# Opening of a fused attention block: order of the rotated key's copies, of the latent evictions, and eight extra matmuls at the start

## The chip, the cores and the metric

The kernel runs on one core of one Trainium2 chip. The metric is the device time of one execution in microseconds (us). Three timed runs of the kernel before the change took 625.54, 625.70 and 627.62 us; the median is 625.70 us. Below, 0.5% of that (3.1 us) is taken as the smallest difference that counts as faster or slower.

## The reference

One decoder layer on 512 tokens with 16 learned meta tokens ahead of them, model width 1024. Two attention branches of 16 heads run on the same normed input and are merged by gates:

```
u = rmsnorm(h, pre_norm_g[l])
proj = u @ w_in[l]
(cq, ckv, k_pe_raw, z_mla, fq, fk, fv, f_logit, z_fox, gate_a, gate_b) = jnp.split(proj, split_idx, axis=-1)
q = (rmsnorm(cq, ...) @ w_uq[l])...          # per head 64 plain + 32 rotary
kv = (rmsnorm(ckv, ...) @ w_ukv[l])...       # per head 64 key + 64 value
k_pe = rope(k_pe_raw, pos)[:, None]          # one rotated key for all heads
q_m = jnp.concatenate([q_nope, rope(q_pe, pos)], axis=-1)
k_m = jnp.concatenate([k_nope, broadcast k_pe], axis=-1)
o_mla = causal_block_attention(q_m, k_m, v_mla, MLA_SCALE)
log_f = log_sigmoid(f_logit + fox_forget_b); cum = jnp.cumsum(log_f)
o_fox = causal_block_attention(fq, fk, fv, FOX_SCALE, cum)
mixed = (sigmoid(gate_a) * y_mla + sigmoid(gate_b) * y_fox) @ w_out[l]
h = h + rmsnorm(mixed, post_norm_g[l])
```

## The kernel before, in words

Every float32 product is made of three passes in float32r: each operand is split into a high half and a low half, and high x high, low x high and high x low are summed in PSUM. So each weight block of 128x1024 goes through three steps: a DMA into `wraw` (three buffers), a copy of the high half on ScalarE (`wh`, line 127), and a subtraction on GpSimd (`wl`, line 102). Each result leaves PSUM the same way: ScalarE copies the high half, VectorE subtracts the low one (`split_lo`, line 102).

The work has an opening, sixteen attention stages (head pairs, forgetting branch and latent branch in turn) whose gaps are filled with projections, a merge, and an output product. Only the opening is touched. TensorE's order is written out by hand; the other four engines' orders come from a scheduler that follows priorities, and each engine runs its list strictly in order.

The opening, for five row tiles t (four of 128 tokens, and tile 4 of 16 meta tokens): load `ht`; sum of squares and scale into `hn`; transpose on TensorE (`pt`, by `turn`, line 351) and evict as `uTh` (ScalarE, line 372) and `uTl` (VectorE, line 369). `small` (line 387) multiplies with the narrow weights `wsh`/`wsl` into `psm` (cq, ckv, raw rotary key, forget logits). `back` (line 399) norms that and rotates the key into `sm`. `latent` (line 424) transposes `sm` on TensorE into `pc`, **of which there is one buffer**, and empties it by four evictions: `cTh` (ScalarE, line 433), `cTl` (VectorE, line 434 through 102), `kpT` (the rotated key, ScalarE, line 435) and `fT` (forget logits, ScalarE, line 436). The next tile's `pc` transposes wait for all four.

Then come, in TensorE's order: the forgetting branch's first queries `fq` and keys `fk` (two halves), the first rotary queries `ppe` (two halves, from cTh/cTl), the first values `v` (two halves), four steps of a gate `pg`, and the first scores `st`. These products take turns on three PSUM banks (`accp`), so each starts only once the result three before it has left: the second `ppe` waits for the first `hlk` (VectorE's split of `fk`), and `v` waits for the second `hlk`.

Beside that, VectorE has: `hlq` and `hlk` (splits of fq, fk); `KPH`, four copies of the rotated key to four partition groups (line 560), and `KPL`, two subtractions (line 563 through 102); the forget sums `fa` (lines 506 and 507, the scan) and `ch` (line 511), which go by DMA into `CT`, an operand of the first scores; the rotation products `pt<-ppe` (line 623); the values' maxima `vsc` and splits `vh` (lines 668 to 690); and `sf`, the masked scores out of PSUM (line 755). The first scores have four `st` banks; after four tiles they wait for `sf`. GpSimd has the `wl` splits, the setup of `maskt`, `vh`, `pn` and `KPL` (lines 545 to 561), and the rest of the rotation of ppe (lines 628 to 631), whose casts into `gT` take the memory in which `kpT` and `ch` lay, so they wait for the last reader of `kpT`.

Of the kernel before, what the change touches and what calls it, by code (L numbers as in the profile page):

```python
# [23 lines left out]
S = 512  # L24
META = 16
L = S + META
NH = 16
# [27 lines left out]
def block_kernel(ctx: ExitStack, tc: tile.TileContext, x, meta_tokens, pre_norm_g, w_in, fox_forget_b,  # L55
# [45 lines left out]
    def split_lo(eng, lo, src, hi):  # L101
        eng.tensor_tensor(out=lo, in0=src, in1=f32(hi), op=ALU.subtract)  # L102
# [158 lines left out]
    with ExitStack() as ph:  # L261
# [63 lines left out]
        hns, sts, pts0 = {}, {}, {}  # L325
# [73 lines left out]
        def back(t):  # L399
# [6 lines left out]
            for a, b, i in both:  # L406

                nc.scalar.activation(sm[:rows, a:b], psm[:rows, a:b], AF.Square, scale=(b - a) ** -0.5,
                                     accum_out=st2[:rows, i : i + 1])
# [14 lines left out]
        def latent(t, sm):  # L424
# [8 lines left out]
            nc.scalar.copy(cTh[:, i0:3, ds], pc[:, i0:3, :rows])  # L433
            split_lo(nc.vector, cTl[:, i0:3, ds], pc[:, i0:3, :rows], cTh[:, i0:3, ds])
            nc.scalar.copy(kpT[:, ds], pc[0:ROPE, 3, :rows])
            nc.scalar.activation(fT[:, ds], pc[ROPE : ROPE + NH, 3, :rows], AF.Identity, bias=fb)
# [5 lines left out]
        free = lambda ins: ins  # L442
        gps = ppt.tile([128, 4, 128], F32, tag="pt", name="gps")
# [20 lines left out]
        for c in (2, 3):  # L464
# [33 lines left out]
        qk = q_fox(0) + k_fox(0)  # L498
        run(qk[:7])
# [19 lines left out]
        run(qk[7:])  # L519
# [14 lines left out]
    with ExitStack() as att:  # L534
# [24 lines left out]
        for r in range(4):  # L559
            nc.vector.tensor_copy(KP[0][32 * r : 32 * r + 32], kpT)  # L560
        nc.gpsimd.memset(f32(KP[1]), 0.0)
# [3 lines left out]
        gpool = gctx.enter_context(tc.tile_pool(name="gpool", bufs=1, side="right"))  # L565
        gT = [gpool.tile([128, KD, S], F32, tag=n, name=n) for n in ("gT0", "gT1")]
# [25 lines left out]
        def pe_unit(g):  # L592
            if g == 0:
                r0, tt = (p.rearrange("p a b -> p (a b)")[:, 0 : 8 * S].bitcast(F32).rearrange("p (c s) -> p c s", c=4)
                          for p in pts)
            else:
                r0, tt = gT[0][:, 4:8], gT[1][:, 4:8]
            rp = r0[:, 0:2]

            rr = [r0[:, 2:4], tt[:, 2:4]] if g else [t[:, 4:6] for t in gT]  # L600
            if g == 0:
                nc.sync.dma_start(rp, rope_pe)
# [8 lines left out]
            def srcs():  # L611
                if g:

                    tc.keep_in_program_order(nc.sync.dma_start(rp, rope_pe))
                return [wuqh[:, k, 8 * g : 8 * g + 8, NOPE + 16 * x : NOPE + 16 * x + 16]
                        for x in range(2) for k in range(2)]

            for xi in range(2):
                get = (lambda: half(1)) if xi else weights(srcs, lambda ws: half(0, ws))

                def done(i, ps, xi=xi):
                    for cs in range(2):
                        nc.vector.tensor_tensor(out=tt[:, 2 * xi + cs], in0=ps, in1=rp[:, cs], op=ALU.mult)
                out += unit(f"ppe{g}{xi}", get, cq_act, 2, REAL, done)

            def rest(x):

                nc.gpsimd.tensor_tensor(out=tt[:, x], in0=tt[:, x], in1=tt[:, 3 - x], op=(ALU.subtract, ALU.add)[x])
                hi, lo = rr[x][:, 0], rr[x][:, 1]
# [4 lines left out]
                else:  # L634

                    for h in range(2):
                        for i in range(2):
                            r = 64 * h + 32 * i + 16 * x
                            dma(f32(QP[r : r + 16]), rr[x][16 * h : 16 * h + 16, i])

            def store(x, a, b):
                for i in range(2):
                    dma(qpe_dram[8 * g + a : 8 * g + b, i, x], rr[x][16 * a : 16 * b, i])
# [193 lines left out]
        pe, rest0, store0 = pe_unit(0)  # L837
        pe_rest = [(0, lambda x=x: rest0(x)) for x in range(2)]
        g = gate_unit()
        first = pe + v + [(0, in_order)] + g[:4]  # L840
# [23 lines left out]
        run(first)  # L864
# [190 lines left out]
```

## Time and profile before

| what | value |
|---|---|
| median of the three timed runs | 625.70 us |
| profiled execution: span from first to last instruction | 622.1 us |
| median less span (what lies around the instructions) | 3.6 us |
| TensorE busy | 599.9 us, 96% of the span |
| VectorE, ScalarE, GpSimd busy | 315.4, 330.8, 265.5 us |
| TensorE busy in the first 74 us | 62.1 us |
| chain of work that ended last | TensorE 86%, VectorE 5%, ScalarE 4% |

The profile lists no device time of its own for the profiled execution; its span is set beside the timed runs. Times in the trace are us from the span's start. A row of the timeline gives start, duration, engine, line, operation, out<-in, shapes, count, and in brackets the idle time before it and what ended that.

### The profile page before, as it was taken

How to read it: one execution, taken by the hardware profiler on the slowest of the kernel's cores; microseconds unless marked ns; L12 is line 12 of the kernel's file. 1: busy time of each engine (PE TensorE's matmuls, PEld its weight loads, DVE VectorE, ACT ScalarE, POOL GpSimd, SP SyncE). 2: the span in 40 equal slices, each digit the busy share in tenths (PEclk: the TensorE clock that was granted, in tenths of full speed). 3: DMA queues.
4: the chain of work that ended last, by engine and by line, in shares of the span. 5: the costliest groups of instructions: out<-in, count | busy, mean ns of one | idle time of the engine just before them, and what ended most of it. 6: DMA issues, size and time to landing. Idle time of an engine off the chain costs nothing.

```text
span 622.1 us, 11008 instructions
## 1 busy us (share of the span) xinstructions
PE 599.9 (96%) x3811; PEld 507.3 (82%) x3811; DVE 315.4 (51%) x922; ACT 330.8 (53%) x757; POOL 265.5 (43%) x270
## 2 busy tenths in 40 slices
PE   5997999799999999999999999999999999999996
PEld 5886789689889789888888898887888888888885
DVE  3848647555765764674675657627321122024034
ACT  7755745655764864774676657656322222232321
POOL 4307535352346543344443523542744444444610
PEclk9999999899999999999999999999999999999999
DMA  9422589969798787878579697871433332333602
GB/s 289 99 76 53 120 178 142 242 141 190 145 186 161 149 208 154 172 167 204 140 161 174 145 169 159 187 168 40 136 102 101 102 93 79 100 103 115 257 34 102
DMA packets 223512, 89.31 MB, mean 144 GB/s; under 512 B 141708, under 2 KB 216852, under 8 KB 223456
## 3 DMA queue, kind: packets, MB, share of 16 engines
q1 hardware_dynamic: 223456, 88.61, 61.9%
q8 instruction: 30, 0.49, 0.3%
q14 instruction: 26, 0.21, 0.1%
HBM read 54.43 MB, written 4.00 MB: 94 GB/s over the span
## 4 chain that ended last, share of the span: by engine, by line
PE 86%; DVE 5%; ACT 4%; issue 2%; DMA 1%; SPq 0%; POOL 0%; DVEq 0%; ACTq 0%
PE z L96 14%; PE pg L96 14%; PE py L96 14%; PE v L96 9%; PE fq L96 7%; PE po L96 7%; PE fk L96 7%; PE st L96 5%; PE ov L96 3%; PE psm L96 3%; DVE sf L755 2%; PE mq L96 2%; ACT wh L127 2%; PE mk L96 1%; DVE vh L690 1%
## 5 line engine op out<-in xcount | busy, mean ns | idle before, releaser
L102 POOL TENSOR_TENSOR wl<-wraw,wh 128x1024 fp32r<-128x1024 f32 (+1 forms) x90 | 207.3, 2308 | 221.0 <-ACT wh L127 219.2
L127 ACT CAST wh<-wraw 128x1024 fp32r<-128x1024 f32 (+1 forms) x90 | 89.9, 1003 | 172.3 <-issue 47.7
L763 ACT ACTIVATE sf<-sf,nb 128x144 f32<-128x144 f32 (+3 forms) x128 | 72.0, 564 | 15.8 <-DVE nb L755 15.8
L791 DVE SCALAR_TENSOR_TENSOR pn<-sf,ri,pn 128x128 f16<-128x128 f32 (+3 forms) x128 | 68.8, 576 | 13.1 <-ACT pn L790 12.2
L790 ACT ACTIVATE pn<-sf,ri 128x128 f16<-128x128 f32 (+3 forms) x128 | 61.5, 551 | 19.9 <-ACT sf L763 17.9
L938 DVE SCALAR_TENSOR_TENSOR tb<-th,py 128x512 f32<-128x512 f32 x16 | 11.0, 687 | 101.9 <-PE py L96 101.9
L96 PE MATMUL st<-hlk,hlq 64*128 64x272 f32 (+3 forms) x480 | 52.8, 317 | 5.0 <-ACT hlk L239 4.1
L96 PE MATMUL z<-uTh,wh 128*128 128x512 f32 x128 | 50.8, 397 | 0.0
L96 PE MATMUL pg<-uTh,wh 128*128 128x512 f32 x128 | 50.2, 392 | 0.0
L96 PE MATMUL z<-uTh,wl 128*128 128x512 f32 x128 | 50.1, 391 | 0.0
L96 PE MATMUL z<-uTl,wh 128*128 128x512 f32 x128 | 49.9, 390 | 0.0
L96 PE MATMUL pg<-uTh,wl 128*128 128x512 f32 x128 | 49.8, 389 | 0.0
L96 PE MATMUL pg<-uTl,wh 128*128 128x512 f32 x128 | 49.8, 389 | 0.0
L96 PE MATMUL py<-gh,wh 128*128 128x512 f32 x128 | 49.8, 389 | 0.0
L96 PE MATMUL py<-gl,wh 128*128 128x512 f32 x128 | 49.8, 389 | 0.0
L96 PE MATMUL py<-gh,wl 128*128 128x512 f32 x128 | 49.8, 389 | 0.0
L96 PEld LDWEIGHTS st<-hlk,hlq 64*128 64x128 f32 x480 | 37.0, 186 | 15.0 <-ACT hlk L239 5.8
L755 DVE CUSTOM_DVE_ANT_0 sf<-st,maskt 128x272 f32<-128x272 f32 (+2 forms) x128 | 48.4, 434 | 0.9 <-PE st L96 0.8
L777 POOL TENSOR_TENSOR mt<-sf,ri 128x96 f32<-128x96 f32 (+1 forms) x32 | 9.5, 297 | 89.4 <-DVE ri L772 66.5
L96 PE MATMUL v<-uTh,wh 128*128 128x256 f32 (+1 forms) x128 | 36.6, 286 | 2.3 <-DVE hlk L102 2.3
L96 PE MATMUL v<-uTl,wh 128*128 128x256 f32 (+1 forms) x128 | 36.5, 285 | 0.0
L96 PE MATMUL fk<-uTl,wh 128*128 128x256 f32 (+1 forms) x128 | 36.4, 285 | 0.0
(189 smaller groups left out, 1403.3 us busy)
## 6 DMA issues: line engine op xcount, KB each, us to landing
wraw<-in_w_in_dram SPq DMA_DIRECT2D x56, 512.0 KB
wraw<-in_w_br_fox_dram SPq DMA_DIRECT2D x8, 512.0 KB
wraw<-in_w_br_mla_dram SPq DMA_DIRECT2D x8, 512.0 KB
wraw<-in_w_out_dram SPq DMA_DIRECT2D x8, 512.0 KB
pt<-pn SPq DMA_TRANSPOSE x128
xr<-in_x_dram SPq DMA_DIRECT2D x4, 512.0 KB
out_dram<-yo SPq DMA_DIRECT2D x8, 256.0 KB
QP<-qpe_dram SPq DMA_DIRECT2D x7, 256.0 KB
```

Source lines behind the costliest of these rows:

```text
L96: nc.tensor.matmul(*a, **k)
L102: eng.tensor_tensor(out=lo, in0=src, in1=f32(hi), op=ALU.subtract)
L127: nc.scalar.copy(wh[:, :n], raw[:, :n])
L690: nc.vector.scalar_tensor_tensor(out=lo, in0=p, scalar=sc[:, 3:4], in1=hi, op0=ALU.mult, op1=ALU.subtract)
L755: nc.vector.tensor_tensor_reduce(out=sf_of(h, b)[:, c0 : c0 + w], in0=ps[h][:, o : o + w], in1=maskt[:, m0 : m0 + w], scale=-scale, scalar ...
L763: exps[g] = nc.scalar.activation(sf, sf, AF.Exp, bias=sums["nb"][:, h, b : b + 1], scale=-1.0, accum_out=sums["su"][:, h, b : b + 1]).ins
L777: nc.gpsimd.tensor_tensor(out=mt, in0=src, in1=ri.unsqueeze(3).broadcast_to([128, 2, nb_, META]), op=ALU.mult)
L790: nc.scalar.activation(hi, sf, AF.Copy, scale=rib)
L791: nc.vector.scalar_tensor_tensor(out=lo, in0=sf, scalar=rib, in1=hi, op0=ALU.mult, op1=ALU.subtract)
L938: nc.vector.scalar_tensor_tensor(out=tb[br], in0=ths[i, br], scalar=1.0, in1=py, op0=ALU.add, op1=ALU.mult)
```

## The change

1. Eight matmuls `spun` of 128x512 (`ONE` by `CT`, both just zeroed or set by GpSimd) are put ahead of TensorE's first transpose. Their result is not used.
2. In `latent`, the four evictions get a higher priority and another order: `cTh`, `kpT`, `fT`, `cTl`.
3. `KPH` and `KPL` (and with them the release of the opening's last memory and the making of `gT`) move from ahead of the attention stages to behind the `ppe` steps, and are held behind the last rotation product (`issue_after(turned_q[0])`).
4. `run(qk[7:])` (the keys' steps) moves ahead of the code of `ch` and its DMAs, and the copy of `ch` on ScalarE is held behind the second `hlk` copy. `behind` holds weight copies back to after tile 1's squares until `ppe` is through.

```
@@ latent
-            nc.scalar.copy(cTh[:, i0:3, ds], pc[:, i0:3, :rows])
-            split_lo(nc.vector, cTl[:, i0:3, ds], pc[:, i0:3, :rows], cTh[:, i0:3, ds])
-            nc.scalar.copy(kpT[:, ds], pc[0:ROPE, 3, :rows])
-            nc.scalar.activation(fT[:, ds], pc[ROPE : ROPE + NH, 3, :rows], AF.Identity, bias=fb)
+            with tc.high_priority(offset=60):
+                nc.scalar.copy(cTh[:, i0:3, ds], pc[:, i0:3, :rows])
+                nc.scalar.copy(kpT[:, ds], pc[0:ROPE, 3, :rows])
+                nc.scalar.activation(fT[:, ds], pc[ROPE : ROPE + NH, 3, :rows], AF.Identity, bias=fb)
+                split_lo(nc.vector, cTl[:, i0:3, ds], pc[:, i0:3, :rows], cTh[:, i0:3, ds])
...
+        spun = acc("spun")
+        for _ in range(8):
+            mm(spun, ONE, CT[:, 0:512], start=True, stop=True)
         gps = ppt.tile([128, 4, 128], F32, tag="pt", name="gps")
         tps(gps[:, 0, 0:KD], g8, ident[0:KD, 0:KD])
...
         qk = q_fox(0) + k_fox(0)
+        behind[:] = [squared[1]]
         run(qk[:7])
         latent(3, sms[3])
...
+        run(qk[7:])
         ch = pal.tile([NH, 2, L], F32R, tag="ch", name="ch")
-        nc.scalar.activation(ch[:, 0], fa[:, 0], AF.Copy, scale=-1.0 / SC_FOX)
+        with tc.issue_after(halved[("k", 1, 0), 1]):
+            nc.scalar.activation(ch[:, 0], fa[:, 0], AF.Copy, scale=-1.0 / SC_FOX)
...
-        run(qk[7:])
...
-        for r in range(4):
-            nc.vector.tensor_copy(KP[0][32 * r : 32 * r + 32], kpT)
         nc.gpsimd.memset(f32(KP[1]), 0.0)
-        for h in range(2):
-            split_lo(nc.vector, KP[1][64 * h : 64 * h + 32], kpT, KP[0][0:32])
-        lctx.close()
...
-        run(first)
+        run(pe0)
+        behind.clear()
+        with tc.issue_after(turned_q[0]):
+            for r in range(4):
+                nc.vector.tensor_copy(KP[0][32 * r : 32 * r + 32], kpT)
+            for h in range(2):
+                split_lo(nc.vector, KP[1][64 * h : 64 * h + 32], kpT, KP[0][0:32])
+        lctx.close()
+        gpool = gctx.enter_context(tc.tile_pool(name="gpool", bufs=1, side="right"))
+        gT += [gpool.tile([128, KD, S], F32, tag=n, name=n) for n in ("gT0", "gT1")]
+        run(first[len(pe0) :])
```

(The rest of the diff defers lookups of `gT` and keeps handles of instructions.) Beside the eight matmuls, TensorE's order is unchanged, and so is SyncE's. The other engines' orders change at the places shown below; behind the first values every engine's order is as before. The numbers behind a tile's name are buffer numbers and differ between the two kernels.

ScalarE where tile 0's `pc` is emptied, before:

```order
L418 COPY sm_365<-psm_253 128x16
L408 ACTIVATE sm_405,st_4_406<-psm_380 16x128
L433 COPY cTh<-pc_418 128x3x128
L322 ACTIVATE st_4_406<-st_4_406,eps_t 16x1
L372 ACTIVATE uTh<-pt_0_427,gcol 128x128
L418 COPY sm_405<-psm_380 16x16
L372 ACTIVATE uTh<-pt_0_427,gcol 128x128 x2
L435 COPY kpT<-pc_418 32x128
L436 ACTIVATE fT<-pc_418,fb 16x128
```

and in the changed kernel:

```order
L418 COPY sm_374<-psm_262 128x16
L434 COPY cTh<-pc_427 128x3x128
L435 COPY kpT<-pc_427 32x128
L436 ACTIVATE fT<-pc_427,fb 16x128
L408 ACTIVATE sm_414,st_4_415<-psm_389 16x128
L372 ACTIVATE uTh<-pt_0_436,gcol 128x128
```

The three evictions now stand together, ahead of tile 4's square and tile 3's `uTh`; on VectorE `cTl` moved up likewise, to directly behind tile 1's two `sm` rows (line 420).

VectorE from the split of fq to the values' maxima, before:

```order
L102 TENSOR_TENSOR hlq_612<-fq_564,hlq_612 128x512
L560 COPY KPH<-kpT 32x528 x4
L102 TENSOR_TENSOR KPL<-kpT,KPH 32x528 x2
L102 TENSOR_TENSOR hlk_646<-fk_621,hlk_646 128x272
L506 TENSOR_SCALAR fa<-fT,fa 16x528
L507 TENSOR_SCALAR fa<-fa 16x528
L102 TENSOR_TENSOR hlk_646<-fk_649,hlk_646 128x256
L623 TENSOR_TENSOR pt_706<-ppe_744,pt_705 128x512
L511 TENSOR_SCALAR ch<-fa,ch 16x528
L623 TENSOR_TENSOR pt_706<-ppe_744,pt_705 128x512
L623 TENSOR_TENSOR pt_706<-ppe_753,pt_705 128x512 x2
L668 TENSOR_REDUCE vsc_796<-v_771 128x1
```

and in the changed kernel:

```order
L102 TENSOR_TENSOR hlq_612<-fq_573,hlq_612 128x512
L102 TENSOR_TENSOR hlk_646<-fk_621,hlk_646 128x272
L511 TENSOR_SCALAR fa<-fT,fa 16x528
L512 TENSOR_SCALAR fa<-fa 16x528
L102 TENSOR_TENSOR hlk_646<-fk_649,hlk_646 128x256
L627 TENSOR_TENSOR pt_715<-ppe_741,pt_714 128x512
L518 TENSOR_SCALAR ch<-fa,ch 16x528
L627 TENSOR_TENSOR pt_715<-ppe_741,pt_714 128x512
L627 TENSOR_TENSOR pt_715<-ppe_750,pt_714 128x512 x2
L873 COPY KPH<-kpT 32x528 x4
L102 TENSOR_TENSOR KPL<-kpT,KPH 32x528 x2
L673 TENSOR_REDUCE vsc_805<-v_780 128x1
```

The six `KPH`/`KPL` rows moved from ahead of the first `hlk` to ahead of the values' maxima; nothing else changed places.

GpSimd at the setup of the attention stages, before:

```order
L102 TENSOR_TENSOR wl_735<-wraw_729,wh_734 128x512
L102 TENSOR_TENSOR wl_763<-wraw_738,wh_762 128x1024
L545 MEMSET maskt 128x544
L556 MEMSET vh 128x128
L546 AFFINE_SELECT maskt<-maskt 128x128
L558 MEMSET pn_703 128x2x128 x3
L558 MEMSET pn_704 128x2x128
L561 MEMSET KPL 128x528
```

and in the changed kernel:

```order
L102 TENSOR_TENSOR wl_732<-wraw_726,wh_731 128x512
L551 MEMSET maskt 128x544
L562 MEMSET vh 128x128
L552 AFFINE_SELECT maskt<-maskt 128x128
L564 MEMSET pn_712 128x2x128 x3
L564 MEMSET pn_713 128x2x128
L565 MEMSET KPL 128x528
L102 TENSOR_TENSOR wl_772<-wraw_735,wh_771 128x1024
```

The setup now stands ahead of the weight split for `v` (`wl_763` before, `wl_772` now). On ScalarE that weight's copy `wh` moved correspondingly from directly behind the last `cTh` to behind the first `fa` row.

More of the change, by code (lines that the diff above doesn't have):

```diff
@@ L101, in split_lo @@
     def split_lo(eng, lo, src, hi):
-        eng.tensor_tensor(out=lo, in0=src, in1=f32(hi), op=ALU.subtract)
+        return eng.tensor_tensor(out=lo, in0=src, in1=f32(hi), op=ALU.subtract)
     def wload(srcs):
@@ L558, in block_kernel @@
             nc.gpsimd.memset(pn[b // 3][:, :, PN_STEP * b % 15, :], 0.0)
[L559 to L560 removed]
         nc.gpsimd.memset(f32(KP[1]), 0.0)
[L562 to L566 removed]
+        gT, turned_q = [], []
         wuqh = wuq.rearrange("p k (h e) -> p k h e", e=NOPE + ROPE)
```

40 lines of the change are left out of this document (22 added, 18 removed).

## Prediction

> **What bounds the kernel now.** First the page's head and its chain of waits: TensorE is the bound nearly everywhere.
>
> ```profile
> span 622.1 us, 11008 instructions
> PE 86%; DVE 5%; ACT 4%; issue 2%; DMA 1%; SPq 0%; POOL 0%; DVEq 0%; ACTq 0%
> ```
>
> So a change in the opening pays what it moves the point from which TensorE runs on, and no more. The second view is TensorE's waits in the first 90 us, each row giving the total, the number and the longest.
>
> ```profile
> PE pc L99 <- ACT fT L436: 1.1, 1, 1.1
> PE ppe L96 <- DVE hlk L102: 1.5, 1, 1.5
> PE v L96 <- DVE hlk L102: 2.3, 1, 2.3
> ```
>
> These three waits, 4.9 us, are what parts 2 and 3 of the change aim at. Behind the first scores all orders are as before and the work waits on itself, so I take a shift at the first scores to reach the end whole: span 622.1 + 3.6 around it = 625.7, and every gain below is taken from that.
>
> **Eight matmuls at the start.** The third view is TensorE's timeline at the first `psm` product, and the windows around the one long pause later on.
>
> ```profile
> 12.74 0.52 PE L96 MATMUL psm<-wsh,uTh 128*128 128x432 f32 x1
> 13.10 0.36 PE L96 MATMUL psm<-wsh,uTl 128*128 128x432 f32 x1
> 13.29 0.36 PE L96 MATMUL psm<-wsh,uTh 128*128 128x432 f32 x1
> ...
> 8.87 2.17 ACT L372 ACTIVATE uTh<-pt,gcol 128x128 fp32r<-128x128 f32 x8
> 18.00 0.75 DVE L348 TENSOR_SCALAR hn<-ht,st 128x1024 f32<-128x1024 f32 x1
> 19.61 1.63 PE L99 MATMUL pt<-ident,hn 128*128 128x128 f32 x16
> 112.00:115.40 3.40, 0.09 (x4) 0.05 (x2) 0.06 (x1) 1.32 (x2) 0.29 (x1) 1.00 1.19 276
> 115.40:119.00 3.60, 3.60 (x20) 2.00 (x22) 2.61 (x13) 2.98 (x12) 2.08 (x1) 0.53 1.06 274
> ```
>
> Starts are 0.36 us apart up to 13.10 and 0.19 after it: half speed, then full. The last two rows show the same clock later: TensorE stands 3.3 us, and in the next stretch the granted clock is 0.53. The eight matmuls are to have this start-up behind them. Saved at most 8 x 0.17 = 1.3 us on `psm`; but what follows `psm` are the transposes of tile 2, which need `hn`, done at 18.75 by VectorE, whose own chain from the first `uTh` does not move. They now start at 19.61, so 18.80 is the earliest: **0.8 us**. The cost: at half speed a 512-column product takes 0.36 x 512/432 = 0.43 us (estimate from the rows), eight take 3.4 us, and the first transposes move from 5.93 to about 7.2; `uTh`, which needs them, starts only at 8.87 behind a load, so this is covered, with some 0.5 us to spare. Bounds: -0.3 (cover gone by a little) to +0.8.
>
> [...]
>
> **Latent evictions first.** Tile 0's `pc` is emptied by cTh, kpT, fT, and cTl, with tile 3's work between.
>
> ```profile
> 27.72 0.45 ACT L433 CAST cTh<-pc 128x384 fp32r<-128x384 f32 x1
> 30.31 0.36 ACT L436 ACTIVATE fT<-pc,fb 16x128 f32<-16x128 f32 x1
> 29.44 0.53 DVE L102 TENSOR_TENSOR cTl<-pc,cTh 128x384 fp32r<-128x384 f32 x1
> 29.27 0.36 PE L96 MATMUL psm<-wsl,uTh 128*128 128x432 f32 x1
> 30.73 0.44 PE L99 MATMUL pc<-ident,sm 128*128 128x128 f32 x2 [1.10 <-ACT fT L436]
> 31.10 2.16 DVE L369 SCALAR_TENSOR_TENSOR uTl<-pt,gcol,uTh 128x128 fp32r<-128x128 f32 x8
> ```
>
> With kpT and fT (0.24 and 0.36) right behind cTh, fT ends near 28.7; cTl then is last, at about 29.57 (moved ahead of tile 4's five small operations, 0.4 us). The next `pc` starts at 29.62 instead of 30.73: **1.1 us**. What is late next: tile 3's products want the fourth `uTl` at 32.5; it starts some 0.3 us earlier than its 31.10 and four take 1.1, so there is no new wait. Bounds: 0.5 to 1.1.
>
> **Rotated key's copies behind the rotary queries.** From here on I keep the clock of the old trace; the 1.9 us gained so far shift all of it.
>
> ```profile
> 47.23 2.27 DVE L560 CAST KPH<-kpT 32x528 fp32r<-32x528 f32 x1
> 50.20 0.53 DVE L560 CAST KPH<-kpT 32x528 fp32r<-32x528 f32 x1
> 52.04 1.41 DVE L102 TENSOR_TENSOR KPL<-kpT,KPH 32x528 fp32r<-32x528 f32 x2 [0.77 <-POOL KPL L561]
> 53.48 0.44 DVE L102 TENSOR_TENSOR hlk<-fk,hlk 128x272 fp32r<-128x272 f32 x1
> 53.84 2.41 DVE L506 SCALAR_TENSOR_TENSOR fa<-fT,fa 16x528 f32<-16x528 f32 x1
> 56.28 1.25 DVE L507 TENSOR_TENSOR_SCAN fa<-fa 16x528 f32<-16x528 f32 x1
> 57.45 0.39 DVE L102 TENSOR_TENSOR hlk<-fk,hlk 128x256 fp32r<-128x256 f32 x1
> 58.37 0.69 DVE L511 SCALAR_TENSOR_TENSOR ch<-fa,ch 16x528 fp32r<-16x528 f32 x1
> ...
> 46.18 2.39 POOL L102 TENSOR_TENSOR wl<-wraw,wh 128x1024 fp32r<-128x1024 f32 x1 [14.19 <-ACT wh L127]
> 48.52 0.55 POOL L545 MEMSET maskt<- 128x544 bf16 x1
> 51.47 0.54 POOL L561 MEMSET KPL<- 128x528 f32 x1
> 53.13 2.56 POOL L102 TENSOR_TENSOR wl<-wraw,wh 128x1024 fp32r<-128x1024 f32 x1 [1.13 <-ACT wh L127]
> 61.58 2.54 POOL L628 TENSOR_TENSOR pt<-pt 128x512 f32<-128x512 f32 x2
> ...
> 49.77 0.39 ACT L239 CAST hlk<-fk 128x272 fp32r<-128x272 f32 x1
> 51.47 0.65 ACT L505 ACTIVATE fa<-fa 16x528 f32<-16x528 f32 x1
> 52.02 1.03 ACT L127 CAST wh<-wraw 128x1024 fp32r<-128x1024 f32 x1
> ```
>
> Read the long rows. A KPH takes 0.53, but 2.27 beside `wl` (46.18 to 48.57) and the memset behind it; L506 has the size of L511 (0.69) but takes 2.41 and ends 0.56 after `wl` (53.13 + 2.56 = 55.69). A VectorE operation that reads only SBUF stands while GpSimd works through one instruction. GpSimd waits likewise: that `wl` ends 2.24 after the last KPL, at 53.45. Operations that read PSUM (hlk, 0.44) do not stand.
>
> Now step by step. Without KPH and KPL, the first hlk follows its ScalarE half at 50.2 instead of 53.5, and `ppe`'s wait of 1.5 goes. L506 follows ScalarE's logarithm (52.12) and ends at 52.9, the scan at 54.1, the second hlk at 54.5: `v` may start at **54.5 instead of 57.9**. That is 3.4 us, if GpSimd's next `wl` (it waits for the copy that ends at 53.05) comes after the scan's start at 52.9.
>
> Then it is given back. That `wl` runs behind the scan to 54.1 + 2.24 = 56.4, and `ch`, ready at 55.1, stands until then: 56.9. Three rotation products of 0.6 follow, to 58.75. The next `wl` now comes 3 us earlier too, 56.4 to 59.2, and the first KPH stands: it ends at 59.6. GpSimd then has its two rotations L628 (1.27 each) ready, and VectorE and GpSimd take turns: 1.12 for GpSimd (1.27 less the 0.15 by which 2.24 falls short of 2.39), 0.40 for a KPH (0.53 less 0.13), twice, to 62.2. There GpSimd must stop, since its casts into gT wait for the last reader of kpT; two KPH and two KPL (0.40 + 0.53 + 1.40) end at 64.5. Only then come the values' maxima.
>
> ```profile
> 64.04 0.42 DVE L668 TENSOR_REDUCE vsc<-v 128x1 f32<-128x256 f32 x1 [2.43 <-PE v L96]
> 66.07 1.02 DVE L690 SCALAR_TENSOR_TENSOR vh<-v,vsc,vh 128x16 f16<-128x16 f32 x3 [0.78 <-ACT vh L687]
> 67.92 0.31 DVE L755 CUSTOM_DVE_ANT_0 sf<-st,maskt 128x144 f32<-128x144 f32 x1 [0.83 <-PE st L96]
> ```
>
> Both maxima (0.86, less 0.06 of overlap) end at 65.3; from 64.46 to the end of vh at 67.09 it is 2.63 us, so `sf` starts at 67.9, against 67.92 before. TensorE, 3.4 us ahead, has its four score banks full by 65.6 and waits there for `sf`. **The three waits are exchanged for one: 0.0 us.** Bounds: with no turns taken (KPH and KPL in one run from 59.2) `sf` starts at 66.0, +1.9; with the setup late (below) -3.3. I take the middle because the rows above show the standing on both sides.
>
> **Sum.** 0.8 + 1.1 + 0.0 = 1.9; 625.7 - 1.9 = **623.8 us**.
>
> **The rivals.**
> *The start-up does not stick*: 0 for the first term, 625.7 - 1.1 = 624.6. For it: the pause of 112 to 115. Against: the transposes between. Chance 0.2.
> [...] Chance 0.18.
> *The setup is in the way, and it ends slower*: GpSimd's setup took 48.52 to 52.01, 3.5 us, and now stands ahead of `v`'s split (2.39). If it starts at 46.3 or later, that split runs past 52.15 and L506 stands; the next split, ready at 53.1, then passes ahead of the scan. If it starts at 48.5 as before: split to 54.4, L506 to 55.0, split to 57.2, scan to 58.3, `v` at 58.7; ch, the rotations and the turns with L628 follow as above, each 2.5 to 3.3 later, and `sf` starts at 71.2: 625.7 - 1.9 + 3.3 = 627.1. I expect a start near 45.7, behind the last fT, because fT moved ahead of a weight copy; the point lies only 0.6 us away. If the split merely passes ahead of the scan (a margin of 0.2 us), `sf` starts at 69.5: 625.4. Chance of either 0.15.
> The change does do what it says: all three waits lose their cause.
>
> **How the numbers follow.** Forecast 623.8, chance 0.37; the rivals 0.2, 0.18, 0.15; 0.1 for anything else, half on each side. The range goes from 621.5 (the open port) to 627.2 (the late setup) and leaves out about 0.1 to 0.15. With 0.5%, or 3.1 us, as about the least that a measurement can tell from no change: faster 0.2 (the open port and half a rest), slower 0.04, same 0.76.
>
> **What would show it.** Starts of `psm` products 0.19 apart from the first on and tile 2's transposes near 18.8: first term right. The second `pc` about 0.1 us behind its cTl, no wait for fT: second right. `v` near 52.6 (54.5 less 1.9), KPH rows longer than 1 us, L628 between them, and a new wait of TensorE in the scores for `sf` of 2 to 3 us: third right. KPH at 0.53 throughout with `sf` near 64 would make the forecast too slow; L506 or the scan over 2 us would make it too fast; and an altered order behind the first scores, or a long pause that moves into a half-clock stretch, would break the assumption that the shift reaches the end.

## The result and the profile after

The changed kernel takes 624.1 us (median of 16 runs, 622.6 to 626.0) against 626.4 us for the kernel before (16 runs, 624.5 to 627.6): **0.9973 of the time, with a 95% interval of 0.996 to 0.9985**. That is 1.7 us less by this ratio (the two medians are 2.2 apart); the forecast was 1.9 less, 623.8 us. By the bound of 0.5% it counts as the same. The size came out right, but one step behind it did not hold. The profile gives the first sign of it: the profiled execution of the changed kernel is not shorter than that of the kernel before (622.4 against 622.1 us), though part of that lies in the two executions and not in the kernels, as shown below.

The page's head and its chain of waits, of the changed kernel:

```profile
span 622.4 us, 11027 instructions
...
PE 87%; DVE 6%; ACT 3%; issue 2%; DMA 1%; POOL 0%; SPq 0%; DVEq 0%; ACTq 0%; POOLq 0%
```

TensorE bounds it as before. TensorE's waits in the first 125 us (total, number, longest):

```profile
PE st L96 <- ACT hlk L239: 3.1, 1, 3.1
PE st L96 <- DVE nb L760: 2.9, 1, 2.9
PE spun L96 <- POOL ONE L226: 2.8, 1, 2.8
PE pt L99 <- DVE hn L348: 0.7, 1, 0.7
PE v L96 <- DVE hlk L102: 0.4, 1, 0.4
```

The three waits that the change aimed at (pc 1.1, ppe 1.5, v 2.3) are gone but for 0.4 at v. One new wait has come, 2.9 us in the scores for the maxima (nb). The 3.1 us for hlk, near 112 us, was there before with 3.3.

The start, in TensorE's timeline (start, duration, operation; the wait in brackets); the first row is of the kernel before, the others are of the changed one:

```profile
10.44 0.71 PE L96 MATMUL psm<-wsh,uTh 128*128 128x432 f32 x1
...
2.84 3.78 PE L96 MATMUL spun<-CT,ONE 128*128 128x512 f32 x8 [2.84 <-POOL ONE L226]
7.49 3.63 PE L99 MATMUL pt<-ident,hn 128*128 128x128 f32 x16 [0.67 <-DVE hn L348]
10.82 0.50 PE L96 MATMUL psm<-wsh,uTh 128*128 128x432 f32 x1
11.15 0.35 PE L96 MATMUL psm<-wsh,uTl 128*128 128x432 f32 x1
11.35 0.36 PE L96 MATMUL psm<-wsh,uTh 128*128 128x432 f32 x1
18.84 1.63 PE L99 MATMUL pt<-ident,hn 128*128 128x128 f32 x16
```

psm starts 0.38 us later than before (10.82 against 10.44). From the second product on it runs at 0.20 us per product, and tile 2's transposes start at 18.84 instead of 19.61: 0.77 earlier, against a forecast of 0.8.

The latent evictions of tile 0 on ScalarE and VectorE, and the second pc on TensorE:

```profile
27.34 0.36 ACT L436 ACTIVATE fT<-pc,fb 16x128 f32<-16x128 f32 x1
28.26 0.54 DVE L102 TENSOR_TENSOR cTl<-pc,cTh 128x384 fp32r<-128x384 f32 x1
28.86 0.66 PE L99 MATMUL pc<-ident,sm 128*128 128x128 f32 x4
```

cTl ends last, at 28.80, and the next pc follows 0.06 us later, at 28.86 instead of 30.73: 1.87 earlier, which is the 0.77 and the 1.1 of the second term.

The rotary part, on VectorE, GpSimd and TensorE; the last row is of the kernel before:

```profile
49.99 0.70 DVE L511 SCALAR_TENSOR_TENSOR fa<-fT,fa 16x528 f32<-16x528 f32 x1 [1.51 <-ACT fa L510]
50.79 1.25 DVE L512 TENSOR_TENSOR_SCAN fa<-fa 16x528 f32<-16x528 f32 x1
52.88 1.92 DVE L518 SCALAR_TENSOR_TENSOR ch<-fa,ch 16x528 fp32r<-16x528 f32 x1
56.53 4.16 DVE L873 CAST KPH<-kpT 32x528 fp32r<-32x528 f32 x4
60.70 1.41 DVE L102 TENSOR_TENSOR KPL<-kpT,KPH 32x528 fp32r<-32x528 f32 x2
62.14 0.78 DVE L673 TENSOR_REDUCE vsc<-v 128x1 f32<-128x272 f32 x2
65.40 0.30 DVE L760 CUSTOM_DVE_ANT_0 sf<-st,maskt 128x144 f32<-128x144 f32 x1
...
50.98 6.08 POOL L102 TENSOR_TENSOR wl<-wraw,wh 128x1024 fp32r<-128x1024 f32 x2 [2.37 <-ACT wh L127]
57.03 2.92 POOL L633 TENSOR_TENSOR pt<-pt 128x512 f32<-128x512 f32 x2
...
52.41 0.39 PE L96 MATMUL v<-uTh,wh 128*128 128x272 f32 x1 [0.40 <-DVE hlk L102]
...
57.90 0.39 PE L96 MATMUL v<-uTh,wh 128*128 128x272 f32 x1 [2.28 <-DVE hlk L102]
```

v starts at 52.41 (forecast 52.6, before 57.90). Then ch takes 1.92 beside the weight split, the four KPH take 4.16 beside the split's end and GpSimd's rotations, and sf starts at 65.40 against 67.92 before: 2.5 us earlier.

And here those 2.5 us go. The columns of a window are its limits, its length, the busy time of TensorE, its weight loads, VectorE, ScalarE and GpSimd (with instructions), the granted clock (1.00 is full speed, 0.50 half speed), and the DMA share and rate:

```profile
62.20:65.60 3.40, 1.02 (x14) 0.67 (x10) 2.54 (x10) 1.80 (x4) 3.37 (x5) 0.99 0.00 0
65.60:72.40 6.80, 6.28 (x24) 4.98 (x25) 5.42 (x27) 6.17 (x20) 3.78 (x10) 0.50 0.35 78
113.40:120.10 6.70, 5.41 (x36) 3.30 (x36) 3.04 (x15) 5.47 (x18) 3.34 (x5) 0.50 1.21 268
```

TensorE stands for most of 62.2 to 65.6, and for the 6.8 us behind it the granted clock is 0.50; the pause near 112 is followed by 6.8 us more, where the kernel before had 3.4. (This last difference is not shown to be the change's: that pause, of 2.6 to 3.9 us, stands in the kernels with parts of the change too, and the stretch behind it is 3.4 us in the profiled executions of a_no_spun and a_no_keys and 6.8 in those of b_spun and b_latent.) The next table follows the same TensorE product through the profiled executions: its start, less its start in the kernel before.

```
product that starts in   after  b_spun  b_latent  b_latent  b_keys  a_fill  a_turn
the kernel before at                                _ch                      _fill
 20.0 us                 -0.77   +0.53    +0.48    -0.20    +0.17   +0.01   -1.01
 40.1                    -1.87   +1.10    -0.60    -1.30    +0.17   -1.10   -2.12
 60.1                    -5.49   +1.10    +2.43    -0.07    -3.16   -4.72   -5.74
 80.1                    -0.41   +1.09    +3.17    +0.07    +1.78   -1.79   -4.75
100.0                    -0.41   +1.09    +3.17    +0.07    +1.78   -1.76   -4.75
125.2                    +0.29   +1.77    +5.18    +1.74    +2.71   -2.05   -6.09
616.2                    +0.30   +1.75    +5.22    +1.76    +2.72   -2.03   -6.01
```

(The other columns are the experiments below.) Two things are to be read. From 125 us to the end no column moves by more than 0.1 us, so everything is decided in the first 125 us, as assumed. And the changed kernel is 5.5 us ahead at 60 us, 0.4 ahead at 80 and 0.3 behind at 125. Of the 2.5 us that sf was ahead, 2.1 are gone at 80 us, behind the new pause.

### The profile page after: what moved, and what is told of

Read it like the earlier page. It is cut to its first block, busy times and chain, and to the rows that moved or that the text cites. A ratio compares the mean times of both kernels' runs of the same rounds, so it can differ in the third digit from the quotient of the medians.

```text
span 622.4 us, 11027 instructions
## 1 busy us (share of the span) xinstructions
PE 605.5 (97%) x3819; PEld 511.6 (82%) x3819; DVE 315.0 (51%) x922; ACT 330.0 (53%) x757; POOL 265.7 (43%) x270
## 3 DMA queue, kind: packets, MB, share of 16 engines
q1 hardware_dynamic: 223456, 88.61, 60.3%
## 4 chain that ended last, share of the span: by engine, by line
PE 87%; DVE 6%; ACT 3%; issue 2%; DMA 1%; POOL 0%; SPq 0%; DVEq 0%; ACTq 0%; POOLq 0%
PE py L96 14%; PE z L96 14%; PE pg L96 14%; PE v L96 8%; PE fq L96 7%; PE po L96 7%; PE fk L96 7%; PE st L96 5%; PE ov L96 3%; PE psm L96 3%; DVE sf L760 2%; PE mq L96 2%; ACT wh L127 2%; DVE vh L695 1%; PE mk L96 1%
## 5 line engine op out<-in xcount | busy, mean ns | idle before, releaser
L96 PE MATMUL fk<-uTh,wh 128*128 128x256 f32 (+1 forms) x128 | 36.4, 285 | 0.0
```

Of the source, the lines that this page charges most:

```text
L96: nc.tensor.matmul(*a, **k)
```

## The experiments

In the names, b_ is the kernel before with something added, a_ the changed kernel with something altered. All timed runs, with the mean of the span and of the granted clock that each run lists:

```
kernel        median us  runs  ratio to before    95%               mean span  mean clock
before         626.4      16   1                                      624.0      0.992
after          624.1      16   0.9973   0.996  to 0.9985              622.5      0.989
b_spun         626.4      12   1.0011   0.9993 to 1.003               624.6      0.990
b_latent       627.3      12   1.0029   1.0016 to 1.0042              625.6      0.991
b_keys         626.5      12   1.0016   0.9999 to 1.0033              624.4      0.989
b_latent_ch    625.0      12   0.9984   0.9971 to 0.9998              623.2      0.992
a_no_spun      624.3      12   0.9972   0.9955 to 0.999               622.6      0.991
a_no_keys      627.5      12   1.0024   1.0005 to 1.0044              625.8      0.991
a_fill         621.6       6   0.9939   0.9919 to 0.9959              619.7      0.995
a_late         630.2       7   1.006    1.0039 to 1.0082              628.5      0.989
a_late_fill    633.7       6   1.0108   1.0084 to 1.0132              631.7      0.988
a_hold         624.3      12   0.997    0.9953 to 0.9986              622.4      0.989
a_hold_fill    621.7       6   0.9929   0.991  to 0.9948              619.9      0.995
a_turn_fill    618.1       6   0.9875   0.9849 to 0.99                616.6      0.998
```

The time of before is that beside the changed kernel; its span and clock are means over the 87 runs beside the experiments (medians there 625.6 to 626.5), and every ratio is to the runs of before on the same chip. Within one kernel the span goes with the clock: the 17 runs of before at 0.996 have a mean time of 624.0 us, the 17 at 0.989 one of 627.1. Straight lines of one common slope, with a height of its own for each kernel, give 0.38 us for each 0.001 (runs scatter by 0.76 around them). Where "at equal clock" is said below, this slope is used to bring spans to 0.996: before 622.6, after 619.7. It is an estimate: the slope is 0.45 among the runs of before alone and 0.29 among those of after, which makes the 2.9 us between the two 3.1 or 2.5. Listed clocks count the time ahead of the first recorded rise, some 6 to 15 us, as full, although products there can run at half speed (psm in the kernel before, 0.36 us apart up to 13.10), so they do not show what the eight products do.

### b_spun: the eight products alone

```diff
+        spun = acc("spun")
+        for _ in range(8):
+            mm(spun, ONE, CT[:, 0:512], start=True, stop=True)
```

> The kernel before with only the eight products ahead of the first transpose. If the first term is real, psm products are 0.19 us apart from the first on, tile 2's transposes start at 18.8 instead of 19.6, and all behind them is 0.8 us earlier: 0.9988 of the time before. If the gain is lost again further on (in the wait for the score maxima, or in a stretch at half clock), the ratio is 1.000 though the psm rows are full speed.

Measured: 1.0011 (0.9993 to 1.003), and 0.2 us less than before at equal clock. No gain is shown. Its profiled execution shows why one trace can't settle it: there hn for the second half of the first transposes came 1.6 us late, and tile 2's transposes started at 20.14. Over the profiled executions of all kernels, that product starts on average 0.34 us earlier than in before's trace with the eight products (nine kernels, -1.01 to +0.53) and 0.25 later without (five, -0.20 to +0.82): 0.6 us apart, with a scatter as large.

### b_latent: the latent order alone

```diff
+            with tc.high_priority(offset=60):
                 nc.scalar.copy(cTh[:, i0:3, ds], pc[:, i0:3, :rows])
-            split_lo(nc.vector, cTl[:, i0:3, ds], pc[:, i0:3, :rows], cTh[:, i0:3, ds])
                 nc.scalar.copy(kpT[:, ds], pc[0:ROPE, 3, :rows])
                 nc.scalar.activation(fT[:, ds], pc[ROPE : ROPE + NH, 3, :rows], AF.Identity, bias=fb)
+                split_lo(nc.vector, cTl[:, i0:3, ds], pc[:, i0:3, :rows], cTh[:, i0:3, ds])
```

> The kernel before with only the order of the latent evictions changed (kpT and fT ahead of cTl, all four raised). If the second term is real, the second pc starts 1.1 us earlier (29.6) and the end comes 1.1 us earlier: 0.9982 of the time before. If it is taken up by a later wait, the second pc starts at 29.6 and the ratio is 1.000.

Measured: 1.0029 (1.0016 to 1.0042), slower than before. The 1.1 us are there (the column of the table goes from +0.48 at 20 us to -0.60 at 40), and at 60 us it is 2.4 us behind. ScalarE in the kernel before, then ScalarE and TensorE in this one:

```profile
52.95 0.35 ACT L239 CAST hlk<-fk 128x256 fp32r<-128x256 f32 x1
57.56 0.64 ACT L510 ACTIVATE ch<-fa 16x528 fp32r<-16x528 f32 x1 [4.25 <-DVE fa L507]
...
51.13 1.03 ACT L127 CAST wh<-wraw 128x1024 fp32r<-128x1024 f32 x1
56.75 0.64 ACT L511 ACTIVATE ch<-fa 16x528 fp32r<-16x528 f32 x1 [4.59 <-DVE fa L508]
57.30 0.34 ACT L239 CAST hlk<-fk 128x256 fp32r<-128x256 f32 x1
...
58.51 0.59 PE L96 MATMUL v<-uTh,wh 128*128 128x272 f32 x1 [3.67 <-DVE hlk L102]
```

In the kernel before, ScalarE wrote hlk at 52.95 and ch at 57.56. Here the raised evictions turned the two around: ch waits 4.6 us for the scan with hlk behind it in the same queue, and v waits 3.7 us instead of 2.3, and half clock follows (v's first product takes 0.59 instead of 0.39; the clock record has 0.50 from 57.3 to 64.2).

### b_keys: the key's copies alone

The whole change without spun and without the latent order.

> The kernel before with only the rotated key's copies moved behind the rotary queries (and what goes with that: the weight copies held behind the squares, ch behind its half). My theory: v starts 3 to 5 us earlier, TensorE then waits 2 to 3 us for sf, sf comes 0.6 us earlier than before, and the granted clock falls to 0.5 for 3.4 to 6.8 us behind that wait, which costs 1.7 us or more: ratio 1.000 to 1.003. The rival, that the move itself carries the gain (sf earlier, clock unchanged), gives 0.996 to 0.999.

Measured: 1.0016 (0.9999 to 1.0033), as the theory had it; at equal clock 0.7 us less than before. Its waits hold the new row, as in the changed kernel:

```profile
PE st L96 <- DVE nb L756: 2.9, 1, 2.9
```

sf starts at 67.78 against 67.92, in an execution that began 0.17 us later, and the clock is at 0.5 for 6.8 us twice (67.6 and 115.4, by the trace's clock record). The move takes 3.3 us off v and gets a pause and the first of these stretches for it; the second stands in b_spun and b_latent too, without the move.

### a_fill: the pause before sf filled

```diff
+            def pause(n):
+                idle = ovp.tile([128, 512], F32, tag="ov", name=f"idle{si}")
+                for _ in range(n):
+                    mm(idle, ONE, CT[:, 0:512], start=True, stop=True)
-            for fn in [s0] + late + [s1]:
+            for fn in [s0] + ([lambda: pause(13)] if si == 0 else late) + [s1]:
                 fn()
```

> The changed kernel with thirteen more products of zeros (512 columns, 0.21 us each at full clock, 2.8 us) ahead of the scores' second half in the first stage, where TensorE stands 2.9 us for sf; no result is changed and nothing waits for them. If the pause is what drops the clock, there is no half-clock stretch at 65 to 72 us, the products behind sf (st, pg, z) run at full speed, and the time falls by about 1.9 us against the changed kernel: 0.994 of the time before. If half-clock stretches come whatever TensorE does there, the stretch at 65 us stays and the time is that of the changed kernel, 0.997.

(The products are not of zeros at that point, since CT holds the sums by then; nobody reads them. The thirteen take 3.30 us, from 63.90.) Measured: **0.9939 (0.9919 to 0.9959)**, 2.1 us less than the changed kernel by the two ratios (0.0034 of 625). sf itself is no earlier; the windows behind it and behind the second pause:

```profile
66.80:73.60 6.80, 6.69 (x38) 5.11 (x37) 4.59 (x20) 5.69 (x19) 2.54 (x6) 1.00 0.36 81
113.40:116.70 3.30, 3.30 (x18) 1.86 (x20) 2.56 (x13) 2.73 (x11) 2.04 (x1) 0.50 1.02 279
```

The clock stays at 1.00 behind sf, and the stretch at 113 is 3.4 us long. At equal clock a_fill and the changed kernel are alike (619.3 and 619.7). The scores wait for sf as long as they did; what the fill takes away is the clock's price: shown. Its size is about 2.1 us; the two intervals together allow 0.6 to 3.6, and the changed kernel's own trace gave 2.1.

### a_no_spun and a_no_keys: one part left out

a_no_spun takes the three lines of spun out of the changed kernel; a_no_keys is the kernel before with spun and the latent order.

> The changed kernel without the eight products (latent order and key move together). The sum of these two alone, from the runs so far, is a loss: 1.0029 and 1.0016 make 1.0045. My theory now is that they are not to be added: the latent order alone lets GpSimd's setup start early, beside the key's copies and ahead of the next weight split, and with the copies moved away that collision is gone. Then the second pc starts 1.1 us earlier, L511 takes 0.7 instead of 2.4 and v starts 4.5 us earlier than before; and the eight products are worth their 0.8 us: 0.9985 to 0.999 of the time before. If the eight products are worth nothing, the time is the changed kernel's, 0.997; if the losses add, 1.004.

Measured: 0.9972 (0.9955 to 0.999), the changed kernel's own ratio. The latent order alone is slower, the key move alone is not faster, and the two together are faster, so the ratios do not add. The eight products are again not seen at the end; at equal clock they are worth 0.9 us (620.7 against 619.7), but the mean clock is 0.991 without them and 0.989 with them. Whether they cause that is not settled: the interval of 0.17% on each side covers a gain of 0.8 us.

> The changed kernel with the key's copies back at their old place (eight products and latent order together, copies ahead of ch). If the collision explains the loss of the latent order alone, it is here too: GpSimd's setup starts behind fT near 44.5, the copies take 5 us instead of 4, TensorE waits 3 us or more at v, and the time is 1.001 to 1.003 of that before. If the terms are independent, as I forecast, it is 0.997.

Measured: 1.0024 (1.0005 to 1.0044). The forecast's independence of the terms is refuted: two parts that the forecast priced at 1.9 us together lose. TensorE's wait at v:

```profile
PE v L96 <- DVE hlk L102: 3.9, 1, 3.9
```

### b_latent_ch: which collision it was

The two expectations above blame GpSimd's early setup. This run takes the latent order alone and adds one thing of the third part, ch behind the second half of hlk:

```diff
+        run(qk[7:])
         ch = pal.tile([NH, 2, L], F32R, tag="ch", name="ch")
+        with tc.issue_after(halved[("k", 1, 0), 1]):
             nc.scalar.activation(ch[:, 0], fa[:, 0], AF.Copy, scale=-1.0 / SC_FOX)
...
-        run(qk[7:])
```

> The kernel before with the latent order and one thing more: ch on ScalarE is held behind the second half of the first keys, as in the changed kernel. In the run with the latent order alone ScalarE took ch (which waits for the scan) ahead of that half, hlk came at 57.30 instead of 52.95 and v at 58.5. If that turn of the order is the whole loss, v now starts about 1.1 us earlier than in the kernel before, with a wait of 2.3 as there, and the time is 0.998 to 0.999 of that before. If the loss lies in GpSimd's early setup beside the copies, v stays late and the ratio is 1.002 or more.

Measured: 0.9984 (0.9971 to 0.9998), 1.0 us less than before. The setup still starts at once behind fT (44.37) and KPH still takes 5.00 beside it, so that theory of mine falls; the order on ScalarE was the loss. The copies and v in this kernel:

```profile
45.52 5.00 DVE L562 CAST KPH<-kpT 32x528 fp32r<-32x528 f32 x4
...
56.40 0.39 PE L96 MATMUL v<-uTh,wh 128*128 128x272 f32 x1 [2.26 <-DVE hlk L102]
```

That is 1.50 earlier than before, of which 0.20 is the start of this execution. In this execution it does not last: the clock is at 0.50 from 56.9 to 60.3, and the table has it level with before from 60 us on. The timed runs, with the mean clock of before, keep 1.0 us. So the second term is about the 1.1 us of the forecast, but only with a line that stands in the third part.

### a_late: the copies behind the first stage's maxima

```diff
-        with tc.issue_after(turned_q[0]):
-            for r in range(4):
-                nc.vector.tensor_copy(KP[0][32 * r : 32 * r + 32], kpT)
...
                 run(fill[:5])
-                run(vts[1, 0] + pe_rest)
+                run(vts[1, 0])
+                with tc.issue_after(sfmin[0]):
+                    for r in range(4):
+                        nc.vector.tensor_copy(KP[0][32 * r : 32 * r + 32], kpT)
...
+                run(pe_rest)
```

(sfmin holds the last maximum of the stage's scores; KPL, the release of kpT's room and gT move along.)

> The changed kernel with the key's copies put behind the score maxima of the first stage (VectorE's queue then has nothing between the rotations and the values' maxima); the casts of the rotated queries and the loads into QP go behind them, still 15 us ahead of their first use. If the copies are what holds sf, sf starts near 62.2 instead of 65.4, TensorE's pause of 2.9 us and the half-clock stretch behind it are gone, and the time is 0.989 to 0.991 of that before. If something else holds sf (the values' maxima behind ScalarE, GpSimd's rotations), sf stays above 64.5 and the ratio is 0.996.

Measured: 1.006 (1.0039 to 1.0082), a clear miss in the sum though the step was right: sf starts at 62.62, and TensorE is 5.3 us ahead at 80 us. Then it is 4.1 us behind at 100. VectorE, the queue that issues DMAs, and a row of TensorE's waits:

```profile
62.62 0.31 DVE L760 CUSTOM_DVE_ANT_0 sf<-st,maskt 128x144 f32<-128x144 f32 x1 [0.94 <-PE st L96]
66.40 1.76 DVE L886 CAST KPH<-kpT 32x528 fp32r<-32x528 f32 x4
...
70.36 6.19 SPq L90 DMA_DIRECT2D QP<-gT  x8
78.75 11.66 SPq L90 DMA_TRANSPOSE pt<-pn  x8
...
PE ov L96 <- DMA pt<-pn: 5.4, 2, 4.8
```

The loads into QP wait for GpSimd's casts, which wait for KPL. They stand in the queue ahead of the eight transposes of the probabilities, which in the changed kernel start at 72.19 and here at 78.75; GpSimd's late work also stands in the way of the probabilities themselves (its last row of pn starts at 78.84, against 72.0 in the changed kernel). TensorE then waits 4.8 us for them and runs slower behind that (25 products ov take 3.61 us from 92.44, where 26 take 1.97 in the kernel before); later it waits 4.0 us more for CT. The useful row is the second: with GpSimd idle from 60.98 to 69.71, four KPH take 1.76 us.

### a_late_fill

The same, with the thirteen products ahead of the third stage's scores.

> As the kernel with the copies behind the first stage's maxima, and thirteen products of zeros (2.8 us) ahead of the third stage's scores, where TensorE stands about 3 us for a half of the keys behind a weight load. Nothing waits for them. If a stretch at half clock costs what its length says (half of 3.4 to 6.8 us), the granted clock stays full from about 13 us to the end of the last product and the time is 1.3 to 2 us less than without them: 0.986 to 0.988. If a later pause brings the stretch instead, or the load comes later by as much, the ratio is that without them.

Measured: 1.0108 (1.0084 to 1.0132): a fault of the experiment. TensorE waited 4.6 us in front of the products. They read CT, which is being loaded anew at that time, and that is the likely cause: the profile names none, but in a_late the scores wait 4.0 us for CT at the same place. The run says nothing on the clock.

### a_hold and a_hold_fill

```diff
+                with tc.issue_after(held[0]) if not g else nullcontext():
                     nc.gpsimd.tensor_tensor(out=tt[:, x], in0=tt[:, x], in1=tt[:, 3 - x], ...
```

(held is the last KPL.) a_hold_fill adds the thirteen products ahead of the third stage's scores, now from `uTh[:, 0, 0:512]`, which is finished since the opening.

> The changed kernel with GpSimd's two rotations held behind the last KPL; nothing else moves, since the casts behind them waited for KPL anyway. If turn-taking with GpSimd is what stretches the copies (4.16 us for four, 1.76 when they ran alone), the three copies behind the weight split take 0.42 each, sf starts near 63.2 instead of 65.4, TensorE's pause falls from 2.9 to 1 us or less, the clock stays full behind it, and the time is 0.990 to 0.992 of that before. If the copies are slow for another reason, sf stays at 65.4 and the ratio at 0.997.

Measured: 0.997 (0.9953 to 0.9986). The edit did nothing: GpSimd does not wait for the last KPL, an instruction of VectorE; its rotations start at 57.59. The copies and the rotations overlap as before:

```profile
57.08 4.16 DVE L874 CAST KPH<-kpT 32x528 fp32r<-32x528 f32 x4
...
57.59 2.92 POOL L634 TENSOR_TENSOR pt<-pt 128x512 f32<-128x512 f32 x2
```

So a_hold is a second measurement of the changed kernel, and gives the same ratio to 0.0003.

> As the kernel with the rotations held, and thirteen products (512 columns, values not used) ahead of the third stage's scores, this time reading only tiles that are finished since the opening, so that nothing is waited for. If the half-clock stretch at 113 us comes from that pause of 3 us, it is gone and the time is 1.3 to 2 us less than with the rotations held alone: 0.987 to 0.989 of that before. If it comes back elsewhere or the products push the scores back, the ratio is that without them or more.

Measured: 0.9929 (0.991 to 0.9948). Against a_hold, which is the changed kernel, the second fill is worth 0.0041, 2.6 us, with intervals of 0.002 on each side; in its trace the clock is at 1.0 from 71.8 us to 617.9. The expected 0.987 to 0.989 built on a_hold's gain that was not there; the fill's own step was 1.3 to 2 us and came out at 2.6.

### a_turn_fill: the rotations held by data

```diff
                 split_lo(nc.vector, KP[1][64 * h : 64 * h + 32], kpT, KP[0][0:32])
+            tq = pts[1].rearrange("p a b -> p (a b)")[:, 0 : 8 * S].bitcast(F32).rearrange("p (c s) -> p c s", c=4)
+            nc.vector.tensor_copy(tq[:, 0:2, 0:1], tq[:, 0:2, 0:1])
```

and the fill of a_hold_fill.

> The kernel before this one in the list did not hold the rotations: its trace shows them at 57.59, ahead of the last key copy, as in the changed kernel, so its time is a repeat of that kernel's. Here they are held by data: behind the last KPL VectorE copies one column of the rotations' input onto itself, and GpSimd has to wait for that. Thirteen products stand ahead of the third stage's scores as in the run with the fill. If turn-taking with GpSimd is what stretches the copies, the four KPH take about 2.1 us instead of 4.16, sf starts near 63.4 by the changed kernel's clock, 2 us earlier, TensorE's pause before it is 1 us or less, the clock stays full behind it and the time is 0.986 to 0.990 of that before. If the copies are slow for another reason, KPH stays at 4.16, sf at 65.4 or later, and the ratio is 0.993 as with the fill alone.

Measured: **0.9875 (0.9849 to 0.99)**, 618.1 us: the fastest kernel of this study. VectorE and GpSimd, TensorE's wait for the maxima, and the windows at the two pauses:

```profile
56.27 2.16 DVE L873 CAST KPH<-kpT 32x528 fp32r<-32x528 f32 x4
58.44 1.41 DVE L102 TENSOR_TENSOR KPL<-kpT,KPH 32x528 fp32r<-32x528 f32 x2
59.87 0.17 DVE L877 COPY pt<-pt 128x2 f32<-128x2 f32 x1
63.19 0.30 DVE L760 CUSTOM_DVE_ANT_0 sf<-st,maskt 128x144 f32<-128x144 f32 x1
...
60.12 2.53 POOL L633 TENSOR_TENSOR pt<-pt 128x512 f32<-128x512 f32 x2 [3.32 <-DVE pt L877]
...
PE st L96 <- DVE nb L760: 1.1, 2, 0.9
...
65.00:72.00 7.00, 6.89 (x39) 5.57 (x36) 6.01 (x20) 7.00 (x21) 4.85 (x11) 1.00 0.37 82
115.00:122.00 7.00, 7.00 (x31) 5.78 (x32) 6.13 (x19) 5.99 (x13) 2.02 (x8) 1.00 1.13 198
```

With GpSimd's rotations behind them the copies take 2.16 instead of 4.16, sf starts 2.0 us earlier relative to KPH's start (6.9 us behind it instead of 8.9), TensorE's longest pause there is 0.9, and the clock is 1.00 through both windows. Turn-taking was what stretched the copies: shown. GpSimd's casts start at 62.60, against 62.23 in the changed kernel (0.6 us later, by an opening that ran 0.24 earlier here), and nobody waits for that.

## Why the prediction was right, and where it was not

- **Eight products, -0.8.** In the profiled execution 0.77: the forecast's size, but not by the forecast's steps. The eight were to cost nothing, "covered, with some 0.5 us to spare"; yet psm starts 0.38 later, behind transposes that run from 7.49 (forecast 7.2) to its start without a gap. The next seven starts of psm take 1.51 us (10.82 to 12.33) instead of 2.66 (10.44 to 13.10): 1.15 gained, less 0.38, is the 0.77. The limit that the forecast set, hn for tile 2, was reached at nearly the same time (18.65), and TensorE does not wait there; that the sum of the two agrees with the forecast's 0.8 is partly luck. Over fourteen executions the gain is nearer 0.6, with a scatter as large. In the timed runs it is not seen (0.9973 with, 0.9972 without).
- **The rival "does not stick".** The changed kernel's profiled execution does not answer it: the first rise in its clock record is at 10.95, when the sixteen transposes are through, so the clock was not full before them. (From 7.5 to 10.8 it ran nothing but transposes, and full clock came at their end; so here they did not keep the clock down.) Other executions with the eight products answer it both ways. In three (a_late, a_hold_fill, a_turn_fill) the clock is full from 6.9 or 7.0 us on and stays so through the transposes. In b_spun it is full from 6.0 to 9.5, at half to 12.9, and full again, with transposes and a wait of 1.6 us in between: there it did not stick. In the other five, the changed kernel's among them, the first rise comes at 10.95 to 12.4 us, against 12.5 to 14.6 in the five executions without the products.
- **Latent order, -1.1.** Right in size and place. What failed is a step that the prediction took silently: that the three terms stand side by side. Alone this part turns ScalarE's order and loses; the hold on ch in the third part undoes that. I had seen that line of the diff and priced only its own place.
- **Key's copies, 0.0.** Each row of the chain came as forecast: v at 52.41 for 52.6, ch standing behind the split, KPH and rotations in turns, a wait of 2.9 for the forecast 2 to 3. The sum was 0.6 us too late, in three steps, each less 1.9 for the shift: KPH began at 56.53 for 56.85, KPL ended at 62.11 for 62.6, sf began at 65.40 for 66.0. KPH and KPL did not run through once begun either: that asked for sf near 64 and KPH at 0.53, and neither is there. No run shows the open port on which the range's 621.5 and the chance of 0.18 rest; in its place the runs showed 4.16 us for the four KPH beside GpSimd's work (after) and 2.16 with the rotations held behind them (a_turn_fill). The late setup did not come either: GpSimd began it at 43.80, as estimated (45.7 less 1.9), and the next split came behind the scan by the estimated 0.2 us (50.98 against 50.79).
- **The step that failed: "a shift at the first scores to reach the end whole".** sf was 2.5 us earlier and the profiled execution ended 0.3 later. The row that should have warned me was among my own: a pause of 3.3 us at 112 and a clock of 0.53 behind it. I forecast a new pause of 2 to 3 us, named half clock as something that would break the sum, and put no price on it. By a_fill it costs about 2.1 us.
- **The base.** "Span 622.1 + 3.6 around it" mixed two things. Every timed run lists 1.8 us around its span. The other 1.8 is that before's profiled execution ran at a mean clock of 0.996, which 17 of 87 runs reach, and those have a mean time of 624.0.

So the 1.9 was met by luck: a gain taken too small and a missing loss cancelled. With the new pause filled, in a_fill, the ratio is 0.9939: 3.8 us less than before, twice the forecast; part of that is that a_fill also runs at a higher mean clock than before (0.995 against 0.992). At equal clock the changed kernel's span is 2.9 us shorter (622.6 to 619.7). The forecast had 1.9; sf in the one trace was 2.5 ahead; where the rest comes from is open, and the choice of slope alone leaves 2.5 to 3.1. The changed kernel's mean clock is lower by 0.0035 (0.9922 to 0.9887), which at 0.38 us per 0.001 takes 1.3 back and leaves 1.6, where the mean spans differ by 1.5. That sum must come out, since the 2.9 was made with the same slope; the independent evidence is a_fill.

In the clock records of the two kernels the stretches at half clock between 13 and 600 us last 3.41 us (before, from 115.48) and 6.83 us (after, from 65.56 and from 113.35), and the first rise to full clock lies anywhere from 6.0 to 14.6 us in the executions of this study. Runs of before list mean clocks of 0.996 and of 0.989, 17 of the 87 each; no trace of before at 0.989 was taken, so the reason is not shown.

## What to carry to other kernels

Price a new pause of TensorE twice: its length, and the half-clock stretch behind it (here 2.9 us, and 6.8 us at 0.50 that cost about 2.1); where the pause can't be removed, fill it with products that nobody reads, on tiles that are long finished (filled, the two pauses here were followed by a clock of 1.00, in a_fill and a_hold_fill). Before adding the terms of a change, look at whether one part turns the order of a queue that another part sets right, on every engine, and run each part alone. Compare timed runs with their granted clock beside them: one profiled execution is one draw, and may be a lucky one.

## What the runs showed of the hardware that was not expected

- A pause of 2.9 us, with TensorE busy for 1.0 of 3.4 us around it, was enough for 6.8 us at clock 0.50 (the changed kernel, a_hold and b_keys), and in a_no_spun and a_hold_fill a like one brought 3.4 us. Even the wait of 2.26 us at v in b_latent_ch was followed by 3.4 us at 0.50; waits of 2.28 in the kernel before and 2.25 in b_spun at the same place were not.
- With no wait of TensorE over 0.9 us behind the start (a_turn_fill, its second pause filled) the clock stayed at 1.00 but for the first 7.0 and the last 1.5 us of the span.
- The same opening differs by up to 1 us between executions (-1.01 to +0.01 at 20 us over the changed kernel, a_fill, a_late, a_late_fill, a_hold, a_hold_fill and a_turn_fill, which share it), with the first rise of the clock (6.9 to 12.4 us) and the arrival of hn; an effect of 0.8 us there can't be read from one trace.
- VectorE's copy and GpSimd's operation in turns: four copies of 32 x 528 take 1.76 us alone, 4.16 beside a split and two rotations, 5.00 beside the setup and a split.
